# A four-layer diffusion trunk on one core: whole runs of small products, RG-LRU work moved off VectorE's conv, and another order for the trunk

## The chip, the cores and the metric

The kernel runs on one core of one Trainium2 chip. The core's engines work side by side, each on its own in-order queue: TensorE (PE, with its weight loads shown apart as PEld), VectorE (DVE), ScalarE (ACT), GpSimd (POOL), and SyncE (SP), which here issues most of the loads. The metric is the device time of one launch, in microseconds, as the median of several executions. A profile shows one execution.

## The reference, cut to what matters

A trunk of four layers over 512 latent and 256 context tokens of width 1024. Layer i has mixer i % 3: gated linear attention (GLA), windowed attention with a sink, RG-LRU, and GLA again. Each layer is modulated by shift, scale and gate from `c @ w_mod`.

```python
for i in range(4):
    kind, j, ctx_out = i % 3, i // 3, i < 3
    shift, scale, gate = split(silu(c) @ w_mod[i] + b_mod[i], 3)         # and the same for c_ctx
    h = rmsnorm(x, g_pre[i]) * (1 + scale) + shift                       # and hc from xc
    if kind == 0: y, yc = mixer_gla(h, hc, ...)     # q, k, v, z; decayed scores in both directions
    elif kind == 1: y, yc = mixer_swa(h, hc, ...)   # softmax over a window of 384, 256 context keys, a sink
    else: y, yc = mixer_rglru(h, hc, ...)           # conv of 4 taps, block-diagonal gates, linear scans
    x = x + gate * rmsnorm(y, g_post[i])            # and xc; every mixer's output is times silu(z), then @ w_out
```

RG-LRU is width 1280 in ten blocks of 128: `u = conv(h @ w_u)`; in each of two directions `r, i = sigmoid(u @ w_ra + b), sigmoid(u @ w_ri + b)`, `a = exp(-8 r softplus(-lam))`, `x = sqrt(1 - a*a) * i * u`, `h_t = a_t h_{t-1} + x_t`; the two directions are summed.

## The kernel before

All values are float32. A big product is made of three: each operand is split into a high part (`wh`, `Rh`, a cast on ScalarE at L265) and a low part (`wl`, `Rl`, a subtraction at L268 on VectorE, or every third time on GpSimd), and PE multiplies high by high, high by low and low by high with 128-row tiles and 256 or 512 columns (L384, L394, L790, L1027). Around them stand smaller products: the modulation (`mod_part`, L521: eight products for 256 columns of `w_mod`, each into 32 of the 128 output rows, so that four lie side by side), broadcasts of a gate (L579), transposes (L539, L635, L1494), GLA's decayed scores by levels of 1 to 128 tokens (L1065, 32 rows by 32 columns), and attention's probabilities times values (`heads`, L1508, 64 output rows for each of the two heads e of a pair).

The code is written for a scheduler that orders each engine's queue by priority (position in the program; `tc.high_priority(n)` moves an instruction ahead by n) and by its estimate of when each instruction can begin. Only the output product and norm of each layer (`finish`, from L731 on) have PE, ScalarE and VectorE in the order written. `weights` keeps two weight pieces converted ahead, in the order of a list per layer; `raw` tiles of 512 KB take each load. `background` puts the next layer's modulation, one piece of 256 columns after the other, between the parts of a layer.

Attention goes by 48 blocks (8 head pairs times 6 query tiles). `scores` makes products, maximum, exponential and normalised probabilities `pe` (VectorE L1465 to L1484, ScalarE L1475). `turn` transposes `pe` into PSUM (L1494) and copies it out to `pt` (L1499), e=0 on ScalarE and e=1 on VectorE. `heads` multiplies by the values. Scores run a block ahead of turns and turns a block ahead of heads; `fill` puts silu gate products (L394) between, by a credit of their length.

RG-LRU (`mix`, once for each block) does: conv on VectorE, one tap as a tensor_scalar (L1582) and three as scalar_tensor_tensor (L1584); split of u (cast L1590, subtraction L1591); load and split of the block's four gate weights (`wgh`, `wgl`); twelve products a stream (L1607); tanh, exponentials and a square root on ScalarE; combinations and scans on VectorE; the sum of the two directions on GpSimd (L1646). `finish` of this layer has two more weight rows of 128 (`wx`, loaded at L765) than the others.

Of the kernel before, what the change touches and what calls it, by code (L numbers as in the profile page):

```python
# [11 lines left out]
F32 = mybir.dt.float32  # L12
# [22 lines left out]
CTX0 = TL  # L35

# [40 lines left out]
def body(ctx: ExitStack, tc: tile.TileContext, I, out, layers=(0, 1, 2, 3)):  # L77
    nc = tc.nc
    V, S, G, PE = nc.vector, nc.scalar, nc.gpsimd, nc.tensor
# [426 lines left out]
    def mod_part(i, n, bank, pool, bufs):  # L506
# [12 lines left out]
        for k in range(KC):  # L519
            g = k % 4  # L520
            PE.matmul(  # L521
                ps[32 * g : 32 * g + 32, 0:256], sT[:, k, :], r2[k // 4][:, k % 4, :],
                start=(k < 4), stop=(k >= 4), skip_group_check=True,
            )
# [230 lines left out]
    def finish(i, kc, extra, last, final, xsrc, xdst):  # L755
# [4 lines left out]
        with phase(f"fin{i}", 6, 0) as fp:  # L760
            if kc > KC:
                wx = [fp.tile([P, kc - KC, D], F32R, name=n) for n in ("wxh", "wxl")]
                for k in range(kc - KC):
                    r = raw()
                    nc.sync.dma_start(r, I["c_w_out"][0, (KC + k) * P : (KC + k + 1) * P, :].rearrange("p (k n) -> p k n", k=4))  # L765
                    f = lambda t: t[:, k, :].rearrange("p (k n) -> p k n", k=4)
                    split(f(wx[0]), f(wx[1]), r)
# [13 lines left out]
            R = (Rh, Rl)  # L781

# [30 lines left out]
            def square(tt):  # L813
                rs[tt] = unit_rstd(fp, xs[tt], y[tt])
# [55 lines left out]
            def way(tt):  # L870

                residual(tt)
                yield
                square(tt)
                yield
                scale(tt)
                yield

# [6 lines left out]
            with tc.manual_schedule(engines={PE.engine, S.engine, V.engine}):  # L885
# [10 lines left out]
                scale(5)  # L896
                step((4, 5), 0)
                next(h)
# [37 lines left out]
    def gla(i, a, ctx_out):  # L936
# [3 lines left out]
        with phase(f"gla{i}") as mp:  # L940
# [96 lines left out]
            def levels(ls, q, Y, X, A):  # L1037
# [11 lines left out]
                small = {8: 0, 4: 1, 2: 2, 1: 3}  # L1049
                for n, L in enumerate(LEVELS):  # L1050
                    dims = ([2 * L, 16 // L], [T + L, 2], [1, L])
                    for gi, chunks in enumerate(groups if L < 128 else ()):
                        at = tl[gi][:, 0, :].rearrange("p (c t) -> p c t", t=P)
                        sml = tl[gi][:, 1, 0:480].rearrange("p (c l t) -> p c l t", l=5, t=32)
# [6 lines left out]
                        for ci, c in enumerate(chunks):  # L1061
                            for g in range(4):
                                t0 = c * P + 32 * g
                                r = slice(32 * g, 32 * g + 32)
                                mm = lambda o, k, x: PE.matmul(o, k, x, start=True, stop=True, skip_group_check=True)  # L1065
                                if L == 1:
                                    mm(sml[r, ci, 4, :], Y[:, 0, t0 : t0 + 32], q[:, t0 : t0 + 32])
                                if L <= 16:
                                    o = at[r, ci, 32 * g : 32 * g + 32] if L == 16 else sml[r, ci, small[L], :]
                                    mm(o, K[:, t0 - k0 : t0 - k0 + 32], view(Xf, t0, dims))  # L1070
                                elif L == 32:
                                    pl, o = (0, 32) if g % 2 == 0 else (1, -32)
                                    mm(
                                        at[r, ci, 32 * g + o : 32 * g + o + 32],
                                        Y[:, pl, t0 : t0 + 32],
                                        X[:, 1 - pl, t0 + o : t0 + o + 32],
                                    )
                                else:
                                    pl, o = (0, 64) if g < 2 else (1, 0)
                                    mm(  # L1080
                                        at[r, ci, o : o + 64],
                                        Y[:, pl, t0 : t0 + 32],
                                        X[:, 1 - pl, c * P + o : c * P + o + 64],
                                    )
# [214 lines left out]
    def attention(i):  # L1299
        with phase(f"att{i}", 6, 0) as mp:  # L1300
# [186 lines left out]

            def turn(b, qt, units, ps, keys):
                pt = mp.tile([P, 2, 640], F32, name="pt", tag="pt", bufs=2)
                for e in range(2):  # L1490
# [5 lines left out]
                    ev = V.tensor_copy if e else S.copy  # L1496
# [6 lines left out]
            def heads(b, qt, units, pt, keys):  # L1503
                po = units[0][0][0]
                kv = b // 2
                for m, t in enumerate(keys):
                    for e in range(2):
                        PE.matmul(  # L1508
                            po[64 * e : 64 * e + 64, 0:P], v[:, t, 64 * kv : 64 * kv + 64],
                            pt[:, e, m * P : (m + 1) * P],  # L1510
# [225 lines left out]
```

## Time and profile before

| | |
|---|---|
| median of 3 runs | 1557.77 us (1557.2 to 1561.75) |
| profiled execution | 1561.59 us |
| its span, first to last instruction | 1559.8 us |
| mean granted PE clock | 0.984 |
| PE busy | 1481.0 us, 95% |
| VectorE, ScalarE, GpSimd busy | 1031.4, 770.7, 238.4 us |
| DMA mean | 104 GB/s |

The profile puts the stages at about: start to 60 us (loads, first modulation); first GLA to 380; output product to 458; attention projections to 540 and attention blocks to 812; output product to 889; RG-LRU to 1138; output product to 1234; last GLA to 1509; last output product to the end. Idle time of an engine that is not the one waited for costs nothing. On PE an instruction's own duration overlaps the next one's, so what it costs is read from the start of one to the start of the next.

### The profile page before, as it was taken

The page shows a single profiled execution, that of the slowest core. Times are in us where ns is not written, and L with a number is a line of the kernel's source. Part 1 is how long each engine was busy: PE and PEld are TensorE (multiplying, and loading weights), DVE is VectorE, ACT ScalarE, POOL GpSimd, SP SyncE. Part 2 cuts the span into 40 slices and gives each one's busy share as a digit, 9 for nine tenths or more (in the row PEclk, how much of TensorE's full clock was granted, in tenths as well). Part 3 has the DMA queues.
Part 4 walks back from the last instruction along what each step waited for, and adds up shares of the span by engine and source line. Part 5 has one row for each costly group of instructions (what it writes and reads, how often), then busy time and mean ns, then how long its engine had stood idle before and what let it go on. Part 6 is the DMA issues. An engine that isn't in the chain of part 4 may idle for free.

```text
span 1559.8 us, 29164 instructions
## 1 busy us (share of the span) xinstructions
PE 1481.0 (95%) x11691; PEld 1222.5 (78%) x11691; DVE 1031.4 (66%) x1912; ACT 770.7 (49%) x1523; POOL 238.4 (15%) x322
## 2 busy tenths in 40 slices
PE   6998999999999999999999998899989999999998
PEld 3777787888878777888788776788867777888886
DVE  5575656576364398787882678999852566766754
ACT  5634352534252366565552556766732465255342
POOL 2211100112121200101001312212211201101011
PEclk8999999999999999999999999999999899999999
DMA  9431324112574532121225633221141233111122
GB/s 303 144 117 59 118 77 139 55 33 88 196 231 132 174 97 62 34 73 47 64 81 180 224 114 109 71 69 57 51 173 58 100 116 111 46 58 55 59 101 89
DMA packets 153047, 162.36 MB, mean 104 GB/s; under 512 B 12418, under 2 KB 141968, under 8 KB 152912
## 3 DMA queue, kind: packets, MB, share of 16 engines
q1 hardware_dynamic: 147456, 146.56, 30.5%
q10 hardware_dynamic: 5456, 13.94, 2.5%
q8 instruction: 92, 1.51, 0.4%
q14 instruction: 43, 0.35, 0.1%
HBM read 138.44 MB, written 11.53 MB: 96 GB/s over the span
## 4 chain that ended last, share of the span: by engine, by line
PE 51%; DVE 10%; ACT 5%; DMA 4%; issue 2%; POOL 1%; SPq 1%; POOLq 0%; ACTq 0%; DVEq 0%
PE mxt L790 14%; PE pjt L394 10%; PE pjt L384 7%; PE pjt L1027 4%; PE mxt L1508 3%; PE mxt L1494 2%; DMA raw<-in_w_mod_dram 2%; PE sct L1607 2%; PE mxt L521 2%; PE mxt L1456 1%; PE mxt L1176 1%; DMA bb<-in_b_mod_dram 1%; PE mxt L1439 1%; DVE wl L268 1%; PE mxt L1148 1%
## 5 line engine op out<-in xcount | busy, mean ns | idle before, releaser
L384 PE MATMUL pjt<-Rh,wh 128*128 128x256 f32 (+1 forms) x592 | 199.9, 339 | 7.3 <-DVE Rh L646 5.5
L384 PE MATMUL pjt<-Rl,wh 128*128 128x256 f32 (+1 forms) x592 | 199.0, 337 | 2.1 <-DVE Rl L647 2.0
L384 PE MATMUL pjt<-Rh,wl 128*128 128x256 f32 (+1 forms) x592 | 197.7, 335 | 0.0
L265 ACT CAST wh<-raw 128x1024 fp32r<-128x1024 f32 x118 | 122.4, 1051 | 121.6 <-PE mxt L790 35.2
L268 DVE TENSOR_TENSOR wl<-raw,wh 128x1024 fp32r<-128x1024 f32 x102 | 128.3, 1266 | 78.7 <-ACT wh L265 78.2
L394 PE MATMUL pjt<-Rh,wh 128*128 128x512 f32 (+1 forms) x448 | 161.1, 360 | 0.0
L394 PE MATMUL pjt<-Rl,wh 128*128 128x512 f32 (+1 forms) x448 | 160.7, 359 | 0.0
L394 PE MATMUL pjt<-Rh,wl 128*128 128x512 f32 (+1 forms) x448 | 158.9, 355 | 0.0
L790 PE MATMUL mxt<-wh,Rh 128*128 128x512 f32 x352 | 140.5, 402 | 4.0 <-ACT wh L265 4.0
L790 PE MATMUL mxt<-wl,Rh 128*128 128x512 f32 x352 | 138.7, 394 | 0.0
L790 PE MATMUL mxt<-wh,Rl 128*128 128x512 f32 x352 | 138.6, 394 | 0.0
L384 PEld LDWEIGHTS pjt<-Rh,wh 128*128 128x128 f32 x592 | 113.0, 191 | 23.1 <-DVE Rh L646 7.1
L384 PEld LDWEIGHTS pjt<-Rl,wh 128*128 128x128 f32 x592 | 113.5, 192 | 16.6 <-DVE Rl L647 4.1
L384 PEld LDWEIGHTS pjt<-Rh,wl 128*128 128x128 f32 x592 | 113.5, 192 | 12.3 <-issue 0.8
L1027 PE MATMUL pjt<-wh,Rh 128*128 128x256 f32 x384 | 112.5, 293 | 0.0
L1027 PE MATMUL pjt<-wl,Rh 128*128 128x256 f32 x384 | 110.2, 287 | 0.0
L1027 PE MATMUL pjt<-wh,Rl 128*128 128x256 f32 x384 | 110.1, 287 | 0.0
L394 PEld LDWEIGHTS pjt<-Rh,wh 128*128 128x128 f32 x448 | 85.0, 190 | 12.5 <-issue 4.5
L394 PEld LDWEIGHTS pjt<-Rh,wl 128*128 128x128 f32 x448 | 85.0, 190 | 11.0 <-issue 3.2
L394 PEld LDWEIGHTS pjt<-Rl,wh 128*128 128x128 f32 x448 | 85.1, 190 | 9.7 <-issue 2.4
L1475 ACT ACTIVATE pe<-mxt,mxs 128x256 f32<-128x256 f32 (+2 forms) x128 | 70.5, 554 | 34.2 <-DVE mxs L1467 29.9
L790 PEld LDWEIGHTS mxt<-wh,Rh 128*128 128x128 f32 x352 | 67.3, 192 | 19.8 <-ACT wh L265 4.8
(299 smaller groups left out, 3530.1 us busy)
## 6 DMA issues: line engine op xcount, KB each, us to landing
rawp<-in_w_mod_dram SPq DMA_DIRECT2D x48, 512.0 KB, 5.8
raw<-in_w_mod_dram SPq DMA_DIRECT2D x48, 512.0 KB, 3.6
raw<-in_a_w_in_dram SPq DMA_DIRECT2D x32, 512.0 KB, 3.5
raw<-in_b_w_in_dram SPq DMA_DIRECT2D x20, 512.0 KB, 4.7
raw<-in_c_w_in_dram SPq DMA_DIRECT2D x20, 512.0 KB, 3.4
xd<-x SPq DMA_DIRECT2D x18, 512.0 KB, 2.6
raw<-in_a_w_out_dram SPq DMA_DIRECT2D x16, 512.0 KB, 3.6
x<-xd ACTq DMA_DIRECT2D x16, 512.0 KB, 9.1
```

The source lines that it names most:

```text
L265: S.copy(h, x)
L268: e.tensor_tensor(l, x, h.bitcast(F32), op=ALU.subtract)
L384: PE.matmul(ps, w[u][:, k, c0 : c0 + P], R[v][:, k, t0 : t0 + n], start=(k == 0 and u + v == 0), stop=(k == KC - 1 and u == 1),)
L394: PE.matmul(ps, w[u][:, k, c0 : c0 + P], R[x][:, k, t0 : t0 + n], start=(k == 0 and u + x == 0), stop=(k == KC - 1 and u == 1),)
L521: PE.matmul(ps[32 * g : 32 * g + 32, 0:256], sT[:, k, :], r2[k // 4][:, k % 4, :], start=(k < 4), stop=(k >= 4), skip_group_check=True,)
L790: PE.matmul(ps, l[:, tt * P : (tt + 1) * P], r, start=(k == 0 and u + v == 0), stop=(k == kc - 1 and u == 1),)
L1027: PE.matmul(ps[:, n, :], R[u][:, k, tt * P : (tt + 1) * P], w[x][:, k, :], start=(k == 0 and u + x == 0), stop=(k == KC - 1 and u == 1),)
L1148: PE.matmul(ps[:, pl * GDV : (pl + 1) * GDV], k[x][:, pl * P : (pl + 1) * P], v[y][:, order[pl][m], :], start=(n == 0), stop=(n == 2),)
L1475: S.activation(p[:, o : o + w], u[e][:, :w], AF.Exp, bias=nm, scale=0.125, accum_out=den[:, n : n + 1],)
L1494: PE.transpose(u[e][:, c * P : (c + 1) * P], ps[e][:, m * P : (m + 1) * P], ident)
L1508: PE.matmul(po[64 * e : 64 * e + 64, 0:P], v[:, t, 64 * kv : 64 * kv + 64], pt[:, e, m * P : (m + 1) * P], start=(m == 0), stop=(m == len( ...
L1607: PE.matmul(ps[:, t0 : t0 + nn], wg[a][:, n, :], x[c][:, p0 : p0 + nn], start=(q == 0), stop=(q == 2),)
```

## The change

The whole body becomes one named block that is ordered by another model of the engines' timelines. The eight modulation products, one level's GLA products and one block's `heads` are each put under `high_priority`, the modulation with the later half of its weights first, GLA's groups and heads' keys in reverse order. `turn` copies both e of a block out on one engine, ScalarE and VectorE in turn from block to block. In `mix`, the first tap and the cast of u go from VectorE to ScalarE, the sum of the directions from GpSimd to VectorE; gate weights are loaded and split one block ahead; while RG-LRU runs, splits are kept off GpSimd. In `finish` the two extra weight rows are loaded after the first output weights instead of ahead of everything, with their split on VectorE; in the one finish that has no fill, one step is drawn a place earlier. An unused function falls away.

```diff
+BURST = 300
...
+    ctx.enter_context(tc.block(name="trunk", schedule_with_timeline_sim=True))
...
-    def split(h, l, x):
+    def split(h, l, x, share=True):
...
-        e = G if cnt[0] % 3 == 0 and not keep_pool else V
+        e = G if share and cnt[0] % 3 == 0 and not keep_pool else V
...
-        for k in range(KC):
-            g = k % 4
...
+        with tc.high_priority(BURST + 200):
+            for n, k in enumerate((*range(4, KC), *range(4))):
+                g = k % 4
+                PE.matmul(
+                    ps[32 * g : 32 * g + 32, 0:256], sT[:, k, :], r2[k // 4][:, k % 4, :],
+                    start=(n < 4), stop=(n >= 4), skip_group_check=True,
+                )
...
-            if kc > KC:
-                wx = [fp.tile([P, kc - KC, D], F32R, name=n) for n in ("wxh", "wxl")]
...
+            def load_extra():
...
+                    split(f(wx[0]), f(wx[1]), r, False)
...
                 w = weights(f"o{kh}")
+                if kc > KC and not kh:
+                    load_extra()
...
+                if not fill:
+                    next(h)
                 step((4, 5), 0)
-                next(h)
+                next(h, None)
...
+                    with tc.high_priority(BURST):
+                        for gi, (chunks, K) in reversed(list(enumerate(Ks))):
+                            products(L, dims, tl[gi], chunks, K)
...
-                    ev = V.tensor_copy if e else S.copy
+                    ev = V.tensor_copy if turns[0] % 2 else S.copy
...
+                with tc.high_priority(BURST):
+                    for m in reversed(range(len(keys))):
+                        for e in (1, 0):
...
+        def gate_weights(b):
+            r = raw()
...
+            split(*gw[b], r[:, :, 0:P])
...
-            V.tensor_scalar(u[:, m], up[:, m], cw[:, 20 + b : 21 + b], cb[:, b : b + 1], op0=ALU.mult, op1=ALU.add)
...
+            with tc.high_priority(120):
+                S.activation(u[:, m], up[:, m], AF.Identity, bias=cb[:, b : b + 1], scale=cw[:, 20 + b : 21 + b])
...
+                S.copy(uh[:, m], u[:, m])
...
+            if b + 1 < RB:
+                gate_weights(b + 1)
...
-            G.tensor_tensor(o, hs[0], hs[1], op=ALU.add)
+            V.tensor_tensor(o, hs[0], hs[1], op=ALU.add)
...
+        keep_pool.append(1)
+        gate_weights(0)
```

In the order's rows a form such as `64x128` is rows by columns of the product, `x7` seven in a row. Line numbers after differ from those before: L521 is L525 after, L394 is L396, L1439 and L1456 (scores) are L1452 and L1469, L1494 is L1510, L1508 is L1526, L579 is L583, L1027 is L1029, L1065 is L1057.

PE in the first GLA, where a modulation piece stands among the products for v (L1027); before:

```order
L1027 MATMUL pjt<-wl,Rh 128x256
L1027 MATMUL pjt<-wh,Rl 128x256
L521 MATMUL mxt<-raw,sT 32x256
L579 MATMUL mxt<-mh,sel 128x256
L521 MATMUL mxt<-raw,sT 32x256 x3
L1027 MATMUL pjt<-wh,Rh 128x256
L1027 MATMUL pjt<-wl,Rh 128x256
L1027 MATMUL pjt<-wh,Rl 128x256
```

and after:

```order
L1029 MATMUL pjt<-wh,Rh 128x256
L1029 MATMUL pjt<-wl,Rh 128x256
L1057 MATMUL sct<-q,Y 32x32
L525 MATMUL mxt<-raw,sT 32x256 x8
L1057 MATMUL sct<-q,Y 32x32
L1029 MATMUL pjt<-wh,Rl 128x256
L1029 MATMUL pjt<-wh,Rh 128x256
```

The products of a piece stand together, with one level product each side; before, they stood in pieces of 4, 1, 3 and the like.

PE in the middle of attention; before:

```order
L394 MATMUL pjt<-Rh,wh 128x512
L1508 MATMUL mxt<-pt,v 64x128
L1494 MATMUL mxt<-ident,pe 128x128 x5
L394 MATMUL pjt<-Rl,wh 128x512
L394 MATMUL pjt<-Rh,wl 128x512
L394 MATMUL pjt<-Rh,wh 128x512
L394 MATMUL pjt<-Rl,wh 128x512
L1508 MATMUL mxt<-pt,v 64x128 x2
L1494 MATMUL mxt<-ident,pe 128x128 x2
L1508 MATMUL mxt<-pt,v 64x128 x7
L1439 MATMUL mxt<-khi,q_6103 128x384
L1439 MATMUL mxt<-klo,q_6103 128x384
```

and after:

```order
L396 MATMUL pjt<-Rh,wh 128x256
L396 MATMUL pjt<-Rl,wh 128x256
L1526 MATMUL mxt<-pt,v 64x128 x10
L1510 MATMUL mxt<-ident,pe 128x128 x2
L1469 MATMUL mxt<-khi,q_6104 128x256
L1469 MATMUL mxt<-klo,q_6104 128x256
L1469 MATMUL mxt<-khi,q_6110 128x256
L1469 MATMUL mxt<-klo,q_6110 128x256
L1510 MATMUL mxt<-ident,pe 128x128 x8
L396 MATMUL pjt<-Rh,wl 128x256
L396 MATMUL pjt<-Rh,wh 128x256
```

A block's heads are one run of ten, and transposes gather in eights.

PE at the end of attention in the new order, from the last fill product on:

```order
L396 MATMUL pjt<-Rh,wl 128x512
L1510 MATMUL mxt<-ident,pe 128x128 x4
L1452 MATMUL mxt<-khi,q_8324 128x384
L1452 MATMUL mxt<-klo,q_8324 128x384
L1458 LDWEIGHTS idb
L1458 MATMUL mxt<-band,idb 128x2x128
L1526 MATMUL mxt<-pt,v 64x128 x10
L1469 MATMUL mxt<-khi,q_8324 128x256
L1469 MATMUL mxt<-klo,q_8324 128x256
L1469 MATMUL mxt<-khi,q_8330 128x256
L1469 MATMUL mxt<-klo,q_8330 128x256
L1510 MATMUL mxt<-ident,pe 128x128 x6
```

and at the end of attention before:

```order
L394 MATMUL pjt<-Rh,wh 128x512
L1494 MATMUL mxt<-ident,pe 128x128 x8
L394 MATMUL pjt<-Rl,wh 128x512
L394 MATMUL pjt<-Rh,wl 128x512
L394 MATMUL pjt<-Rh,wh 128x512
L1494 MATMUL mxt<-ident,pe 128x128 x2
L394 MATMUL pjt<-Rl,wh 128x512
L394 MATMUL pjt<-Rh,wl 128x512
L394 MATMUL pjt<-Rh,wh 128x512
L394 MATMUL pjt<-Rl,wh 128x512
L394 MATMUL pjt<-Rh,wl 128x512
L1508 MATMUL mxt<-pt,v 64x128 x18
```

The last fill product (L396) stands before the last 46 transposes and 34 score products; before, L394 stood up to the last heads.

SyncE's queue in the first 45 us; before:

```order
L275 DMA rawp<-in_a_w_g_dram 128x8x16 x2
L510 DMA rawp<-in_w_mod_dram 128x4x256 x8
L228 DMA rawp<-in_a_w_in_dram 128x4x128 x4
L510 DMA rawp<-in_w_mod_dram 128x4x256 x4
L302 DMA gpt<-in_a_w_g_dram 16x512 x3
L228 DMA raw<-in_a_w_in_dram 128x4x256 x2
L560 DMA gb<-in_g_post_dram 128x256
L564 DMA bb<-in_b_mod_dram 128x256
```

and after:

```order
L277 DMA rawp<-in_a_w_g_dram 128x8x16 x2
L512 DMA rawp<-in_w_mod_dram 128x4x256 x5
L304 DMA gpt<-in_a_w_g_dram 16x512 x3
L230 DMA raw<-in_a_w_in_dram 128x4x256 x2
L564 DMA gb<-in_g_post_dram 128x256
L568 DMA bb<-in_b_mod_dram 128x256
L512 DMA rawp<-in_w_mod_dram 128x4x256 x3
L230 DMA rawp<-in_a_w_in_dram 128x4x128 x4
L512 DMA rawp<-in_w_mod_dram 128x4x256 x4
```

The loads of `gpt`, of 512 KB pieces of `a_w_in`, of `gb` and of `bb` stand ahead of the last seven of `w_mod`.

## Rows read from the trace of the kernel before

**Rows 1.** Windows: length, busy us by engine, PE clock, DMA share, GB/s.

```profile
20.00:45.00 25.00, 20.09 (x161) 10.76 (x150) 16.32 (x39) 13.07 (x26) 6.46 (x6) 0.80 1.07 326
540.00:812.00 272.00, 268.76 (x2063) 218.12 (x2062) 223.10 (x686) 169.54 (x530) 20.00 (x12) 1.00 0.22 60
960.00:1138.00 178.00, 169.37 (x933) 146.99 (x933) 167.97 (x199) 127.34 (x148) 42.88 (x31) 0.98 0.22 66
1157.80:1164.60 6.80, 5.95 (x13) 4.29 (x14) 2.04 (x2) 1.83 (x2) 2.38 (x1) 0.50 0.48 154
```

**Rows 2.** PE timeline, products at L521 and L790: start, us, passes.

```profile
426.50 0.39 PE L790 MATMUL mxt<-wh,Rl 128*128 128x512 f32 x1
426.81 1.07 PE L521 MATMUL mxt<-rawp,sT 128*32 128x256 f32 x16
427.81 0.50 PE L790 MATMUL mxt<-wh,Rh 128*128 128x512 f32 x1
428.16 0.40 PE L790 MATMUL mxt<-wl,Rh 128*128 128x512 f32 x1
...
511.46 0.63 PE L521 MATMUL mxt<-raw,sT 128*32 128x256 f32 x6
512.02 0.39 PE L394 MATMUL pjt<-Rh,wh 128*128 128x256 f32 x1
```

**Rows 3.** PE timeline, attention: start, us, operation, passes.

```profile
620.66 0.43 PE L1508 MATMUL mxt<-pt,v 128*64 128x128 f32 x2
621.02 0.50 PE L394 MATMUL pjt<-Rl,wh 128*128 128x512 f32 x1
621.35 0.39 PE L394 MATMUL pjt<-Rh,wl 128*128 128x512 f32 x1
621.58 0.39 PE L394 MATMUL pjt<-Rh,wh 128*128 128x512 f32 x1
...
625.79 0.38 PE L1494 MATMUL mxt<-ident,pe 128*128 128x128 f32 x2
626.10 0.66 PE L1508 MATMUL mxt<-pt,v 128*64 128x128 f32 x8
626.69 0.50 PE L394 MATMUL pjt<-Rh,wh 128*128 128x512 f32 x1
...
631.26 0.38 PE L1494 MATMUL mxt<-ident,pe 128*128 128x128 f32 x2
631.39 0.47 PE L394 MATMUL pjt<-Rh,wl 128*128 128x512 f32 x1
631.71 0.39 PE L394 MATMUL pjt<-Rh,wh 128*128 128x512 f32 x1
```

**Rows 4.** Lines of VectorE, 540 to 812: busy us, mean ns | idle.

```profile
L1499 DVE COPY pt<-mxt 128x256 f32<-128x256 f32 (+1 forms) x64 | 32.7, 519 | 10.5 <-PE mxt L1494 9.0 <-ACT den L1481 1.1 <-ACT OG L1517 0.2
```

**Rows 5.** Lines of VectorE, 889 to 1138, as rows 4.

```profile
L1584 DVE SCALAR_TENSOR_TENSOR u<-up,cwb,u 128x773 f32<-128x773 f32 x30 | 35.2, 1174 | 0.7
L1582 DVE TENSOR_SCALAR u<-up,cwb 128x773 f32<-128x773 f32 x10 | 8.2, 822 | 0.1
L1590 DVE CAST uh<-u 128x773 fp32r<-128x773 f32 x10 | 5.6, 558 | 2.0 <-PE sct L1607 1.9
```

**Rows 6.** Waits of PE, whole span: us, times, longest.

```profile
PE sct L1065 <- ACT K L1060: 6.4, 6, 2.0
PE mxt L790 <- ACT wh L265: 4.0, 1, 4.0
PE sct L1607 <- POOL wgl L268: 3.6, 1, 3.6
```

**Rows 7.** Tile u, 889 to 1138: ns min/median/max.

```profile
L1584 DVE SCALAR_TENSOR_TENSOR u<-up,cwb,u x30: 1010/1023/2494, 911.7 to 1083.2; 128x773 f32<-128x773 f32 x30
```

**Rows 8.** Chain that ended last: start, us, what.

```profile
1148.11 9.41 DMA raw<-in_c_w_out_dram
```

More of the change, by code (lines that the diff above doesn't have):

```diff
@@ L518, in mod_part @@
         ps = bank()
-        for k in range(KC):
-            g = k % 4
[L521 to L524, printed above, removed]
+        with tc.high_priority(BURST + 200):
[5 more added lines that the diff above has]
+                )
         return ps[:, 0:256]
@@ L760, in finish @@
         with phase(f"fin{i}", 6, 0) as fp:
-            if kc > KC:
-                wx = [fp.tile([P, kc - KC, D], F32R, name=n) for n in ("wxh", "wxl")]
[L763 to L767, printed above, removed]
             parts = [(k, 0, nt) for k in range(KC - 2)]
@@ L781, in finish @@
             R = (Rh, Rl)
+            wx = []
+            def load_extra():
+                wx.extend(fp.tile([P, kc - KC, D], F32R, name=n) for n in ("wxh", "wxl"))
+                for k in range(kc - KC):
+                    r = raw()
+                    nc.sync.dma_start(r, I["c_w_out"][0, (KC + k) * P : (KC + k + 1) * P, :].rearrange("p (k n) -> p k n", k=4))
+                    f = lambda t: t[:, k, :].rearrange("p (k n) -> p k n", k=4)
+                    split(f(wx[0]), f(wx[1]), r, False)
             def product(w, kh, ch, tt, ps):
@@ L1060, in levels @@
                             S.copy(K[:, :kn], view(Yf, k0, ([2 * L, kn // (2 * L)], [T + L, 2], [1, L])))
[L1061 to L1084, printed above, removed]
+                        else:
+                            K = None
+                        Ks.append((chunks, K))
+                    with tc.high_priority(BURST):
+                        for gi, (chunks, K) in reversed(list(enumerate(Ks))):
+                            products(L, dims, tl[gi], chunks, K)
                     if L < 128:
@@ L1486, in scores @@
                 return b, qt, units, ps, loc + [4, 5]
+            turns = [0]
             def turn(b, qt, units, ps, keys):
+                turns[0] += 1
                 pt = mp.tile([P, 2, 640], F32, name="pt", tag="pt", bufs=2)
@@ L1505, in heads @@
                 kv = b // 2
[L1506 to L1510, printed above, removed]
-                            start=(m == 0), stop=(m == len(keys) - 1), skip_group_check=True,
-                        )
+                with tc.high_priority(BURST):
+                    for m in reversed(range(len(keys))):
+                        for e in (1, 0):
+                            PE.matmul(
+                                po[64 * e : 64 * e + 64, 0:P], v[:, keys[m], 64 * kv : 64 * kv + 64],
+                                pt[:, e, m * P : (m + 1) * P],
+                                start=(m == len(keys) - 1), stop=(m == 0), skip_group_check=True,
+                            )
                 o = OG[:, b, qt * P : (qt + 1) * P]
@@ L1576, in gates @@
                 V.tensor_tensor(ex[1][:, m, :], h, ex[0][:, m, :].bitcast(F32), op=ALU.subtract)
+        gw = {}
+        def gate_weights(b):
+            r = raw()
+            for n, (wn, d) in enumerate((("c_w_ra", 0), ("c_w_ri", 0), ("c_w_ra", 1), ("c_w_ri", 1))):
+                nc.sync.dma_start(r[:, n, 0:P], I[wn][0, d, b])
+            gw[b] = [mp.tile([P, 4, P], F32R, name=n, tag=n) for n in ("wgh", "wgl")]
+            split(*gw[b], r[:, :, 0:P])
         def mix(b, up):
@@ L1661, in rglru @@
         gates(RB // 2 - 1, outs)
+        keep_pool.clear()
         finish_args[0] = (RB, ex)
```

60 lines of the change are left out of this document (37 added, 23 removed).

## The prediction

> **What bounds the kernel now.** I read the page from the outside in: the busy shares first, then the windows by stage, then what PE waits for, then PE's own timeline. TensorE is busy for 95% of the span. The windows say the same of the long stages: in the attention stage PE is busy 268.76 of 272 us, in the RG-LRU stage 169.37 of 178 us with VectorE at 167.97 us beside it [rows 1]. So almost everywhere PE's in-order queue sets the end, and in RG-LRU a second engine stands close behind it.
>
> A busy PE is not an efficient PE, and the timeline shows it. I take the time from one row's start to the next row's start. Two like products of 512 columns follow each other in 0.23 us (621.35 to 621.58) [rows 3]. Products of another shape break this. Eight modulation products of 32 columns take 1.00 us as one run (426.81 to 427.81); three of them alone already take 0.56 us (511.46 to 512.02; x6 counts two passes each) [rows 2]. That fits 0.13 us for a run and 0.43 us for each four begun: 0.56 for up to four, 0.99 for eight. The big product ahead of such a run takes 0.31 us instead of 0.23 (426.50 to 426.81), the first behind it 0.35 (427.81 to 428.16) [rows 2]. The products of probabilities with values (heads) take 0.36 us for one (620.66 to 621.02) and 0.59 for four (626.10 to 626.69), so 0.13 a run and 0.23 for each two begun; the first big product behind them takes 0.33 [rows 3]. Two transposes cost 0.31 us ahead of heads (625.79 to 626.10), but 0.13 ahead of a big product (631.26 to 631.39), whose own time is then 0.32 (to 631.71) [rows 3].
>
> **The change part by part.** The matrix products are the same in number and shape; what moves is their order.
>
> *Runs on PE.* I counted runs in both orders. Modulation products: 384 in 82 runs become 384 in 46 (all of 8 or 16), and the fours begun fall from 117 to 96: 36 x 0.13 + 21 x 0.43 = -13.7 us. Steps from a big product to a 32-column one fall from 115 to 82, and as many back: 33 x (0.08 + 0.12) = -6.6. Heads: 352 in 77 runs become 42, pairs begun fall from 197 to 176: 35 x 0.13 + 21 x 0.23 = -9.4. Steps from transposes straight to heads fall from 51 to 13: 38 x 0.18 = -6.8. Steps from heads to big products fall from 53 to 33: 20 x 0.10 = -2.0. Steps from transposes to big products rise from 123 to 141: 18 x 0.09 = +1.6. Together -36.9 us. All of it lies on PE's queue. Finer pricing, by what stands on both sides of each product, gives about -44, which I keep as the far end.
>
> The row at 631.39 shows a big product 0.09 us late behind transposes of the same 128x128 shape [rows 3]. The Trainium skill, TensorEngine Tiling (Array Packing), Key Properties, puts the cost of a switch on a change of the tiling mode, not of the tile. By that alone the +1.6 would be nothing and the sum 1.6 us lower; the row decides for 1.6.
>
> *What attention gives back.* The new order runs the gate products that fill attention earlier. Priced at the steps above, 114 of 138 us of fill are done when 192 of the 352 transposes are, against 86 us before. After the last fill product (third order excerpt), 46 transposes, 34 score products and their heads remain. So from there 22 of 48 blocks run with 24 us of fill instead of 52. PE's own work for a block is (268.8 - 138) / 48 = 2.7 us, hence about 82 us for PE over these blocks. VectorE does 223.1 us in this stage, 4.65 us a block at most [rows 1]; a part of it prepares q, k and weights, so I estimate 4.0 to 4.65, or 88 to 102 us. VectorE would then be late by 6 to 20 us. I take +13, between the ends; 0 if it enters the tail with a lead.
>
> *Start-up.* The excerpt of SyncE's queue shows three small loads, two of 512 KB, and two of 128 KB moved ahead of the last seven w_mod loads, 1.4 MB in all. At the 326 GB/s of that stretch [rows 1] the last w_mod load lands 4.2 us later. Some of its products can trade places with others: +3, between 0 and 4.2.
>
> *GLA levels.* All copies K of a level now precede its products. That can remove waits such as the six, 6.4 us, on K [rows 6]; or, where two levels of a head now stand close together, add as many. I cost it at 0, with ends of -6 and +6.
>
> *RG-LRU.* VectorE loses ten first taps (8.2 us) and ten casts (5.6 us) [rows 5]. It gains ten sums. Their nearest row is the conv step of the same size with two inputs, 1.02 us in the median [rows 7]: +10.2. It gains seven gate-weight splits of 512 columns, by width 0.68 each: +4.8; and three weight splits of 1024, 1.35 each: +4.0. That is +5.2. Against it, the conv steps average 1174 ns [rows 5] with a median of 1023 [rows 7], and the slow ones are those beside a working GpSimd: 30 x 0.15 = 4.5 us that fall away with GpSimd's sums and splits. Other two-input operations suffer alike; at the same 13% on some 60 us more I take 8. Net -7 us, between +1 and -13. ScalarE gains 20 instructions, 0.56 to 1.02 us each by the same rows, 11 to 20 us; at 127 of 178 us [rows 1] it has the room, and loading gate weights one block ahead removes PE's 3.6 us wait for them on GpSimd [rows 6]. I take -7 for the stage. Since VectorE is close to the bound there, some 3 us of the shorter runs of this stage can't show: +3.
>
> *Finish of layer 2.* PE waits 4.0 us for wh on ScalarE [rows 6]; behind it stands a load of c_w_out that took 9.41 us on the chain [rows 8], and then 6.8 us pass at a granted clock of 0.50, which is 1.2 GHz [rows 1], so 3.4 us are lost. With the o0 and o1 loads ahead of the extra rows that wait goes: -7.4 if entirely; I take -6, since the extra rows must still arrive in time.
>
> The eviction of turn, ScalarE and VectorE in alternation instead of side by side, keeps each engine's total; its latency is a rival below.
>
> **Sum.** -36.9 + 13 + 3 + 0 - 7 + 3 - 6 = -31 us. The profiled execution took 1561.59 us, its span 1559.8; so 1530.7 for a like execution. It lay 3.8 us above the median 1557.77, which I take off: 1527 us.
>
> **The rivals.** *VectorE keeps its lead.* If softmax is ahead when the fill runs out, the 13 us are not given back, and start-up hides its loads: 1527 - 16 = 1511; with the finer price of the runs, -7 more, 1504. For it: VectorE has 49 us free in the stage [rows 1]. Against: it can only lead as far as its few buffers reach.
>
> *Attention gives back all its gain, and RG-LRU stands still.* Of the -36.9 some 20 lie in attention (heads, steps around them, a few modulation runs). If VectorE is 20 us late there, not 13, RG-LRU trades VectorE for ScalarE at no gain (+7), and levels cost 6: 1527 + 7 + 7 + 6 = 1547. For it: the new order's tail, plainly bare of fill.
>
> *Slower: turn's evictions hold up the heads.* A turn has 2.67 copies on average, of 519 ns on VectorE [rows 4]. One engine in series needs 1.4 us where two needed 0.7. Heads are hoisted in bursts and may arrive too soon; each of 48 groups then waits up to 1.4 us, 66 us in all, for 1593. The kernel turns slower from 0.75 us a group. Against it: I work out a median of 2.3 us of PE work between a block's transposes and its heads in the new order, with only ten groups below 1.4 us, about 5 us of waiting that the overlap with the other half of the turn shortens. The Trainium skill, TensorEngine Tiling (Array Packing), Performance Considerations, advises both ScalarE and VectorE for emptying PSUM; no run so far shows one turn on one engine.
>
> *The change does not do what it says* is excluded for the runs: the order shows the modulation runs whole. For the waits it is part of the second rival.
>
> **How the numbers follow.** The forecast has 0.53 (about 1514 to 1541), the first rival 0.20 (1504 to 1514), the second 0.18 (1541 to 1555), the third 0.05, anything else 0.04. The range from 1503 to 1550 leaves out the slow cases and a part of the second rival. A measurement of this kernel can tell about 0.3%, 4.7 us, from no change: faster means below 1553.1. The second rival puts 0.04 above that, so: faster 0.87, same 0.06, slower 0.07.
>
> **What would show it.** PE's modulation products in runs of x16 (two passes each) at 1.00 us, and PE busy well below 1481 us at nearly the same share. In attention, waits of PE on VectorE or ScalarE in the last 90 us of the stage, 6 to 20 us. The first w_mod waits some 3 us later. No wait for wgl on GpSimd, conv steps at about 1.02 us on average, ScalarE near 84% in RG-LRU. No 9 us load on the chain at the last finish of layer 2. The prediction is wrong if new waits on pt exceed 20 us, if the w_mod bursts wait for the second half of their weights more than the present runs do, or if the half-clock stretches grow.

## The result and the profile after

The changed kernel takes 1641.07 us in the median (1637.52 to 1641.96) against 1557.49 us for the kernel before: 1.053 times as long, 95% interval 1.050 to 1.056. The forecast was 1527 us, with a range of 1503 to 1550. The span of the profiled execution is 1639.1 us, 79.3 more than before.

The page's first lines after the change (busy us, share of the span, instructions), then those of the same kernel without the block, which comes below:

```profile
PE 1487.6 (91%) x11691; PEld 1249.1 (76%) x11691; DVE 1021.9 (62%) x1913; ACT 787.7 (48%) x1541; POOL 201.1 (12%) x301
```

```profile
PE 1441.5 (95%) x11691; PEld 1207.9 (79%) x11691; DVE 1014.0 (67%) x1913; ACT 786.6 (52%) x1543; POOL 187.9 (12%) x301
```

PE's share fell from 95% to 91%, and yet it is busy 6.6 us longer than the 1481.0 us of before. PE waits more, and more of its work falls into stretches in which its granted clock is at the lower level (0.50, which is 1.2 GHz). This is the table by stage; stages are cut at the first product of the next one on PE's timeline, and each cell gives length / PE idle / time at a granted clock of 0.50, in us:

| stage | before | changed | changed, without the block |
|---|---|---|---|
| start and first GLA | 380.5 / 31.0 / 17.1 | 415.7 / 59.8 / 64.9 | 374.0 / 34.5 / 17.1 |
| attention, projections | 81.1 / 4.9 / 3.4 | 82.4 / 7.1 / 3.4 | 82.2 / 8.6 / 3.4 |
| attention, blocks | 273.4 / 3.2 / 0.0 | 298.9 / 32.6 / 23.9 | 262.2 / 5.7 / 0.0 |
| RG-LRU | 249.1 / 15.0 / 6.8 | 249.5 / 17.3 / 17.1 | 237.1 / 9.0 / 3.4 |
| output of layer 2 | 95.0 / 5.9 / 10.2 | 85.3 / 0.7 / 0.0 | 87.9 / 2.4 / 0.0 |
| last GLA | 275.7 / 11.6 / 10.2 | 301.2 / 27.0 / 35.2 | 272.9 / 12.7 / 6.8 |

The three other stages (output products, 198 us in all) hardly move. In the changed kernel PE idles 144.5 us against 71.7, and 147 us pass at the lower clock against 48. Not all of that time is filled: PE is busy in 116 us of it against 44. If each busy us there loses about half (rows below: 0.21 us for a product instead of 0.12), the clock costs 36 us more. Then 73 us of waits and 36 of clock make 109 us, and the span is 79 longer. The 29 us between are, by this estimate, what shorter runs saved.

The windows of the changed kernel for the stages that lost and of RG-LRU (length, busy us of PE, PEld, DVE, ACT, POOL, then PE clock, DMA share, GB/s), with one stretch of the first GLA; the second row of [rows 1] answers to 575 to 874:

```profile
79.00:416.00 337.00, 296.11 (x3308) 254.03 (x3308) 197.07 (x312) 131.49 (x236) 39.81 (x68) 0.92 0.25 77
575.00:874.00 299.00, 266.29 (x2062) 223.30 (x2061) 230.46 (x697) 172.17 (x532) 20.90 (x12) 0.96 0.21 58
951.00:1201.00 250.00, 232.69 (x1356) 197.90 (x1355) 203.02 (x273) 185.58 (x228) 12.43 (x42) 0.97 0.26 81
1286.00:1588.00 302.00, 274.98 (x2585) 236.49 (x2584) 190.02 (x297) 136.56 (x232) 39.56 (x69) 0.94 0.23 72
265.20:285.70 20.50, 12.70 (x222) 9.01 (x209) 12.44 (x22) 7.46 (x13) 0.00 (x0) 0.50 0.52 164
```

and of the kernel before for its first GLA stage, RG-LRU and its last GLA stage:

```profile
68.00:381.00 313.00, 297.65 (x3365) 252.09 (x3364) 200.04 (x319) 135.23 (x244) 37.65 (x68) 0.99 0.28 86
889.00:1138.00 249.00, 233.95 (x1355) 197.06 (x1354) 223.13 (x276) 168.88 (x208) 58.60 (x62) 0.99 0.27 80
1233.00:1509.00 276.00, 264.37 (x2584) 225.93 (x2583) 188.01 (x295) 133.96 (x233) 35.20 (x69) 0.98 0.25 75
```

These are the largest waits of PE in the whole span after the change (us in total, times, longest). The wait on K was 6.4 us in [rows 6]; the other two rows of that group, the output product's wait for wh and the gates' for wgl, are gone (one of 3.2 us on wgh has come):

```profile
PE mxt L525 <- DMA raw<-in_w_mod_dram: 19.2, 8, 4.0
PE sct L1057 <- ACT K L1091: 10.7, 7, 4.0
PE mxt L681 <- DVE xp L675: 9.8, 1, 9.8
PE mxt L1526 <- DVE pt L1515: 8.6, 3, 4.1
PE mxt L1526 <- ACT pt L1515: 7.2, 4, 2.6
PE pjt L525 <- DMA rawp<-in_w_mod_dram: 5.4, 1, 5.4
```

and two rows of the kernel before that answer to the first and the fourth:

```profile
PE mxt L521 <- DMA raw<-in_w_mod_dram: 7.7, 8, 1.8
PE mxt L1508 <- DVE pt L1499: 0.2, 1, 0.2
```

No row is large. There are many, on loads, on ScalarE and on VectorE alike. The 9.8 us on xp are no new wait: they are the time to PE's first product, and before PE came to the same transposes no earlier (10.58 us against 9.81), after waits of 6.9 and 3.0 us. A piece of PE's timeline in the first GLA shows how they hang together (start, us, operation, passes, in brackets the idle time ahead and what ended it):

```profile
264.50 0.86 PE L1057 MATMUL sct<-X,K 128*32 128x32 f32 x48 [0.95 <-ACT K L1091]
267.49 1.94 PE L525 MATMUL mxt<-raw,sT 128*32 128x256 f32 x16 [2.13 <-DMA raw<-in_w_mod_dram]
269.36 0.69 PE L543 MATMUL mxt<-ident,mp 128*128 128x128 f32 x2
269.98 0.87 PE L1057 MATMUL sct<-X,K 128*32 128x32 f32 x48
274.12 1.94 PE L525 MATMUL mxt<-raw,sT 128*32 128x256 f32 x16 [3.28 <-DMA raw<-in_w_mod_dram]
276.61 0.87 PE L1057 MATMUL sct<-X,K 128*32 128x32 f32 x48
279.87 0.80 PE L1029 MATMUL pjt<-wh,Rh 128*128 128x256 f32 x2 [2.40 <-ACT wh L267]
282.00 0.41 PE L1029 MATMUL pjt<-wh,Rh 128*128 128x256 f32 x1
282.21 0.41 PE L1029 MATMUL pjt<-wl,Rh 128*128 128x256 f32 x1
...
285.91 0.28 PE L1029 MATMUL pjt<-wl,Rh 128*128 128x256 f32 x1
286.03 0.28 PE L1029 MATMUL pjt<-wh,Rl 128*128 128x256 f32 x1
```

Within 20 us four groups of products stand each behind something that is not there yet: a copy K, twice a load of w_mod, a weight cast. The run of eight modulation products takes 1.87 us (267.49 to 269.36) where it took 1.00 in [rows 2], and a product for v takes 0.21 us (282.00 to 282.21) until 285.7, and 0.12 us behind it (285.91 to 286.03). The window row above gives the clock of that stretch as 0.50, the 1.2 GHz level.

SyncE's waits between 235 and 280 us show what the loads stood behind:

```profile
SPq L512 <- PE mxt L525: 43.1, 3, 41.5
```

For 41.5 us the queue held a load whose buffer a modulation product had still to release, and that product stood in PE's order at 260.88 us. The next four loads of w_mod were issued from 261.58 on, and the weights for v behind them. The kernel before has such waits in its first GLA too, 31.0 us the longest; but its longest wait of PE on `raw` of w_mod is 1.8 us.

### The profile page after: what moved, and what is told of

Same layout as the page of the kernel before. It is cut to its first block, busy times and chain, and to the rows that moved or that the text cites. A ratio compares the mean times of both kernels' runs of the same rounds, so it can differ in the third digit from the quotient of the medians.

```text
span 1639.1 us, 29081 instructions
## 1 busy us (share of the span) xinstructions
PE 1487.6 (91%) x11691; PEld 1249.1 (76%) x11691; DVE 1021.9 (62%) x1913; ACT 787.7 (48%) x1541; POOL 201.1 (12%) x301
## 5 line engine op out<-in xcount | busy, mean ns | idle before, releaser
L270 DVE TENSOR_TENSOR wl<-raw,wh 128x1024 fp32r<-128x1024 f32 x105 | 133.9, 1293 | 94.5 <-ACT wh L267 94.3
L396 PE MATMUL pjt<-Rh,wh 128*128 128x512 f32 (+1 forms) x448 | 159.2, 355 | 4.9 <-ACT xq L1394 3.5
L396 PE MATMUL pjt<-Rh,wl 128*128 128x512 f32 (+1 forms) x448 | 157.5, 352 | 0.8 <-DVE wl L270 0.8
L396 PE MATMUL pjt<-Rl,wh 128*128 128x512 f32 (+1 forms) x448 | 157.6, 352 | 0.0
L1029 PE MATMUL pjt<-wh,Rh 128*128 128x256 f32 x384 | 115.0, 301 | 9.3 <-ACT wh L267 4.8
L1029 PE MATMUL pjt<-wh,Rl 128*128 128x256 f32 x384 | 113.9, 297 | 0.0
L1029 PE MATMUL pjt<-wl,Rh 128*128 128x256 f32 x384 | 113.8, 297 | 0.0
L396 PEld LDWEIGHTS pjt<-Rh,wh 128*128 128x128 f32 x448 | 86.6, 193 | 16.1 <-ACT xq L1394 4.3
L396 PEld LDWEIGHTS pjt<-Rh,wl 128*128 128x128 f32 x448 | 86.5, 193 | 10.6 <-DVE wl L270 1.2
L396 PEld LDWEIGHTS pjt<-Rl,wh 128*128 128x128 f32 x448 | 86.6, 193 | 9.4
L1029 PEld LDWEIGHTS pjt<-wh,Rh 128*128 128x128 f32 x384 | 78.2, 204 | 11.1 <-ACT wh L267 5.1
```

Source lines behind the costliest of these rows:

```text
L396: PE.matmul(ps, w[u][:, k, c0 : c0 + P], R[x][:, k, t0 : t0 + n], start=(k == 0 and u + x == 0), stop=(k == KC - 1 and u == 1),)
L1029: PE.matmul(ps[:, n, :], R[u][:, k, tt * P : (tt + 1) * P], w[x][:, k, :], start=(k == 0 and u + x == 0), stop=(k == KC - 1 and u == 1),)
```

## The experiments

All times are medians; ratios are to the kernel before on the same chip, with 95% intervals.

**Which part costs.** Four kernels take the change apart. `no_block` leaves out one line of the changed kernel:

```diff
-    ctx.enter_context(tc.block(name="trunk", schedule_with_timeline_sim=True))
```

> The changed kernel without the named block: the order comes from the model of before, all else stays. If the hoisted runs (modulation, GLA levels, heads) make TensorE wait by themselves, it stays near the changed kernel's 1641 us (1610 to 1645). If the other model of the timeline is the cause, the waits go and the shorter runs show: 1515 to 1545.

Measured: 1525.75 us, 0.981 (0.979 to 0.984). `block_only` puts that line into the kernel before and does nothing else:

> The kernel before with nothing but the named block. If the hoisted runs are the cause, it stays within 10 us of 1557. If the model of the timeline is, it is 1610 to 1640, with PE waits and half-clock stretches in both GLA layers and in attention.

Measured: 1643.80 us, 1.056 (1.053 to 1.058). The first line of its page:

```profile
PE 1513.3 (92%) x11691; PEld 1247.7 (76%) x11691; DVE 1037.5 (63%) x1912; ACT 772.5 (47%) x1521; POOL 247.5 (15%) x322
```

It is long in the stages in which the changed kernel is: the first GLA 410.8 us, the attention blocks 302.7, the last GLA 301.5. PE idles 120.7 us, 49 more than before; by the estimate above the clock costs 24 us more and PE's own work, in this other order, 9. `no_bursts` keeps the block and takes back the hoisted runs:

```diff
-        with tc.high_priority(BURST + 200):
-            for n, k in enumerate((*range(4, KC), *range(4))):
+        for k in range(KC):
...
-                    with tc.high_priority(BURST):
-                        for gi, (chunks, K) in reversed(list(enumerate(Ks))):
...
-                with tc.high_priority(BURST):
-                    for m in reversed(range(len(keys))):
```

> The changed kernel with modulation, GLA levels and heads written as before (no hoisting), block, RG-LRU, finish and the eviction by turns kept. Hoisted runs as the cause: 1540 to 1565. The model of the timeline as the cause: 1620 to 1650.

Measured: 1623.74 us, 1.043 (1.041 to 1.045). `lru_finish_only` is the kernel before with the RG-LRU and `finish` edits:

> The kernel before with only the RG-LRU edits and the moved load of the extra output weights. The stage from the first output product of layer 2 to its end took 85.3 us in the changed kernel against 95.0, the RG-LRU stage 249.5 against 249.1. If these two add up alone, 1545 to 1550; if RG-LRU was held back by the other parts, down to 1535.

Measured: 1544.18 us, 0.992 (0.990 to 0.994). So the loss is that one line's: 87 us on the kernel before, 115 on the changed one. It is the model, not the block: with `schedule_with_timeline_sim=False` in the same block, the program holds the same instructions in the same order on all five queues as without a block, so that kernel was not timed. The rest of the change gains, and the model turns one part of this gain round: the hoisted runs and the eviction by turns bring 18 us without it (1544.18 to 1525.75), and the hoisted runs cost 17 with it (1623.74 to 1641.07). The estimate from above, taken between these last two, says how: the runs save PE 37 us of its own work, but it waits 37 us more (144.5 against 107.9), and the clock costs another 17 (116 busy us at the lower clock against 81).

**What each of the other parts is worth**, taken back one at a time from `no_block`. `nb_no_mod` takes back the modulation runs as above.

> The changed kernel without the block, with the modulation products written as before. By the prediction's price of their runs (13.7 us for the pieces, 6.6 for the steps around them, some 3 of it hidden in RG-LRU) 1540 to 1546 against 1525.75. If a whole run gives back what it saves by waiting for both halves of its weights, it stays within 5 us of 1526.

Measured: 1529.38 us, 0.983 (0.980 to 0.986). The interval overlaps that of `no_block`. The runs did shorten: in 79 runs with 115 fours begun, against 47 and 96, which is 12.3 us by the prediction's price, and 4 more for the steps. But PE idles 7.6 us longer in the first GLA with whole runs (34.5 against 26.9), 2.3 in attention's projections and 1.8 in the last GLA. The waits on w_mod of `no_block`, then of `nb_no_mod`:

```profile
PE mxt L524 <- DMA raw<-in_w_mod_dram: 9.6, 10, 2.2
PE mxt L524 <- DMA rawp<-in_w_mod_dram: 4.1, 1, 4.1
```

```profile
PE mxt L522 <- DMA raw<-in_w_mod_dram: 7.4, 7, 2.0
PE mxt L522 <- DMA rawp<-in_w_mod_dram: 2.5, 2, 2.1
```

A part of the give-back stands in these rows, 3.8 us; the rest is idle time behind other releasers in the same stages. By the estimate from above whole runs save 13 us of PE's own work, 12 more of idle time give that back, and what is left of the difference is mostly clock. `nb_no_heads` takes back the hoisting in `heads`.

> The same without the block, with the heads products not hoisted. The prediction's price of their runs is 9.4 us, 6.8 for transposes ahead of them and 2 behind them: 1540 to 1546. If VectorE takes the stage back, within 5 us of 1526.

Measured: 1543.86 us, 0.991 (0.988 to 0.994), 18 us slower than `no_block`, as priced (the three head terms of the prediction add up to 18.2); the attention stage goes from 262.2 to 278.5 us with PE idle for 5.7 and 5.5. Of 47 steps from transposes straight to heads one is left in `no_block`, and runs of heads fall from 81 to 48. `nb_no_lev` takes back the GLA products.

> The same without the block, with the GLA level products written as before. The prediction costed this part at 0 with ends of -6 and +6, so 1520 to 1532; if the dealt-out products are what speeds up the first GLA stage (374.0 us against 376.6 with the RG-LRU edits alone), 1530 or more.

Measured: 1531.12 us, 0.984 (0.981 to 0.986). The intervals overlap; the two GLA stages are 4.2 and 3.1 us longer than in `no_block`, so a gain of some 5 us is possible and not shown. PE's own work differs by 2 us; most of the rest is time at the lower clock, 44 us against 31, and the granted clock of one kernel differs as much from run to run (0.983 to 0.989 in four runs of `no_block`). `nb_old_ev` takes back the eviction by turns.

```diff
-                    ev = V.tensor_copy if turns[0] % 2 else S.copy
+                    ev = V.tensor_copy if e else S.copy
```

> The same without the block, with both engines emptying one turn as before. If a turn on one engine delays the heads (the rival, up to 1.4 us for each of 48 groups), this is faster by 5 to 20 us, 1506 to 1521, and the waits on pt go. If the distance hides it, 1524 to 1528.

Measured: 1527.48 us, 0.982 (0.979 to 0.985): no difference. Which engine empties a turn does not matter without the block. `nb_mod_dma` hoists the loads of w_mod as far as their products.

```diff
+            with tc.high_priority(BURST + 200):
+                nc.sync.dma_start(
...
```

> The changed kernel without the block, with the loads of the modulation weights hoisted as far as their products. Removing the hoisted modulation products cost 4 us where their runs alone are priced at 16; if the rest is given back in waits for the second half of the weights (16.6 us in all there, 12.4 in the kernel without hoisting), earlier loads take 4 to 10 us off: 1516 to 1522. If the loads are held by their buffers, 1524 to 1530.

Measured: 1527.90 us, 0.981 (0.978 to 0.983). The wait on w_mod into `raw` stays: 9.1 us in ten waits, against 9.6 in ten. Priority is not what holds these loads; they still wait for buffers that modulation products release. SyncE's row from 80 to 410 us, of `no_block`, reads

```profile
SPq L511 <- PE mxt L524: 64.9, 6, 32.0
```

and in `nb_mod_dma` the same wait is 60.4 us in seven, 28.1 the longest.

**Where the finer model costs.** The model that the block's option switches on is called the finer one here. The first try put a block around one layer of `no_block`.

```diff
-            attention(i)
+            with tc.block(name="att", schedule_with_timeline_sim=True):
+                attention(i)
```

> The changed kernel without the block around the trunk, with a block on the finer model around the attention layer alone. If that model's order costs time in every stage whose TensorE work is nearly gapless, by its own order there, the attention stage goes from 262 us to 285 to 300 and the whole to 1550 to 1565, and the GLA and RG-LRU stages stay as they are. If the loss came from what the model did at the start or to the loads ahead, 1526 to 1535.

> The same with the block around the attention layer on the model of before. It prices the edge of a block by itself: 1526 to 1540 by every theory, and the attention blocks near 262 us.

Measured: 1562.07 us with the finer model and 1561.36 with that of before; the stage of the attention blocks 293.1 and 287.3 us. The expectation of the control was missed: a block around one layer costs 36 us without any change of the model. That work on either side of its edges can't mix is the likely reason, which no run shows. Inside these edges the finer model costs 6 us in the stage of the blocks, where it costs 37 around the whole trunk (298.9 against 262.2); the pair can't tell why. `lru_true` does the same around RG-LRU.

> The changed kernel without the block around the trunk, with a block on the finer model around RG-LRU alone. In the kernel with nothing but the trunk's block this stage went from 249.1 to 240.3 us, so the finer order may help where VectorE is the bound: 1515 to 1526. If the loss hits every stage, or the edges cost, 1530 to 1545.

Measured: 1624.87 us, far above both expectations; the RG-LRU stage takes 331.0 us with PE idle for 76.6. Without a control it can't be divided between edges and model.

The second try fixes PE's queue, so that only the other queues differ: `ma_false` and `ma_true` have PE in the code's order through the attention layer, without the trunk's block and with it.

```diff
-            attention(i)
+            with tc.manual_schedule(engines={PE.engine}):
+                attention(i)
```

> The changed kernel without the block, with TensorE's queue in the attention layer in the order of the code; the model orders all else. It is the control of the next. The attention blocks of the code's order run scores, transposes and heads without fill inside a block: 265 to 300 us for the stage, 1530 to 1570 in all.

> The changed kernel with its block, with TensorE's queue in the attention layer in the order of the code. If the finer model costs time by TensorE's order, the attention stage is within 5 us of the control's, the GLA stages stay long (about 412 and 301 us). If it costs time by the order of VectorE's, ScalarE's and the loads' queues, the stage is 15 to 30 us longer than the control's.

Measured: 1614.21 and 1722.46 us. From the first score product to the last of heads both have the same 1796 products in the same order. The control missed its expectation, in all and in the stage, which takes 340.2 us; it takes 368.3 under the finer model. That is 28 us longer, as expected of the other queues, with PE idle 14 us more and 43 us more at the lower clock. In the blocks PE's waits end on VectorE and ScalarE alone, on no load; those on ScalarE grow from 8 to 19 us. `mg_false` and `mg_true` do the same through the GLA layers too.

> Without the block, TensorE's queue in the order of the code in the GLA layers and attention. Control of the next. GLA in the code's order waits for vector work between levels: 400 to 480 us for the first GLA stage.

> With the block, TensorE's queue in the order of the code in the GLA layers and attention. TensorE's order as the cause: both GLA stages within 8 us of the control's. The other queues as the cause: the first GLA stage 20 to 40 us longer than the control's, the last 15 to 30 us.

Measured: 1743.47 and 1812.77 us; attention 343.3 and 372.5, 29 us again; the first GLA stage 454.0 and 471.7, the last 317.7 and 340.9, so 18 and 23 us, where the free orders differ by 42 and 28. The 18 us lie between the two expectations. In GLA some 70 of the first 2755 products still differ at their place. So with PE's products in the same order, or nearly, the finer model still costs 70 us over these three stages, where it costs 107 with free orders; in the first GLA it is less than half. What costs these 70 us is the order of the queues that feed PE. The two figures come from different kernels, so PE's own order may have a part in the rest, and how much is open.

One such place, in `ma_true`. PE waits twice within one turn, first until the other half's exponential has read the PSUM tile that the transposes write, then for that half's normalised probabilities:

```profile
604.82 0.69 PE L1510 MATMUL mxt<-ident,pe 128*128 128x128 f32 x2 [1.97 <-ACT pe L1488]
607.51 1.33 PE L1510 MATMUL mxt<-ident,pe 128*128 128x128 f32 x5 [2.00 <-DVE pe L1497]
```

VectorE has the last maximum that the next exponential needs at 601.15; ScalarE is at two weight casts and a copy of a projection, and VectorE itself at the low part of a weight:

```profile
600.99 0.16 DVE L1480 SCALAR_TENSOR_TENSOR mxs<-mxs 128x1 f32<-128x1 f32 x1
602.35 1.23 DVE L270 TENSOR_TENSOR wl<-raw,wh 128x1024 fp32r<-128x1024 f32 x1 [0.53 <-ACT wh L267]
```

```profile
601.26 2.00 ACT L267 CAST wh<-raw 128x1024 fp32r<-128x1024 f32 x2 [0.42 <-PE pjt L396]
603.16 0.58 ACT L1394 COPY xq<-pjt 128x512 f32<-128x512 f32 x1
603.63 0.58 ACT L1488 ACTIVATE pe<-mxt,mxs 128x384 f32<-128x384 f32 x1
```

The exponential starts 2.5 us after its input is there, and PE's 1.97 us of waiting end with the exponential behind it. In the control the exponential at this place waits 1.98 us for VectorE, and PE's waits in this turn are 0.98, 0.66 and 0.47 us, 2.1 us in all against 4.0. One such place does not show what makes up the 28 us. The last pair tests whether the casts are the cause: `mc_false` and `mc_true` are the two kernels with the weight casts of the attention layer on GpSimd.

```diff
-        S.copy(h, x)
+        (G.tensor_copy if att_on else S.copy)(h, x)
```

> As ma_false (no block, TensorE's attention queue in the order of the code), with the high-part casts of the weights that fall into the attention layer moved from ScalarE to GpSimd. Control of the next: the attention stage near ma_false's 340 us, within 12 us.

> As ma_true (block, the same TensorE order in attention, 368 us there), with the weight casts of the attention layer on GpSimd. In the trace of ma_true two casts in a row (2.0 us) stand ahead of the exponentials that the next transposes wait for. If such casts on ScalarE are what the finer model's order costs, the stage comes within 10 us of the control's. If the rest of the order of VectorE and ScalarE costs it, it stays 20 to 30 us above it.

Measured: 1629.65 and 1721.19 us; the blocks' stage 355.6 and 363.8 us, the projections ahead of it 94.5 and 101.4 (92.7 and 91.9 in the pair before). The gap in the blocks shrinks from 28 to 8 us, but the control rose by 15 us, beyond the 12 expected, and the projections now differ by 7: over both, 27 us became 15. The gap shrank because the control got 17 us longer over both stages; the kernel with the block got 5 us longer, not shorter. So nothing here shows that the casts on ScalarE are what the finer model's order costs. Which instructions on the other queues cost it stays open.

## Why the prediction was wrong

**The step that failed** is the one that is hardly written there: the change of the model itself has no term in the sum. The prediction read the new order on PE, counted its runs, and then priced the queue as if operands came as before, but for one place each: +13 in attention's tail, +3 at the start, 0 (-6 to +6) for the GLA levels. A new order is a new set of waits at every product, on five queues at once. The one line of the block alone, put into the kernel before, costs 87 us (`block_only`). In the changed kernel the waits came to 73 us more and the clock to about 36: attention's blocks idle 29 us more, and the two GLA stages, costed at 0, 29 and 15. No rival had this mechanism; the slow one was sought in turn's evictions. But the prediction's last sentence names three signs of being wrong, and all three came. Waits on pt are 21.8 us in all (0.2 before), waits on w_mod 26.5 (12.3), and the time at the lower clock is 147 us (48).

**The switching term** (-36.9, at the far end -44) had the right sign and was too large: by the estimate above shorter runs saved 29 us in the changed kernel and 30 in `no_block`. In `no_block`, whose runs are other ones, its parts separate: heads 18 us, as priced; the modulation runs some 4 us where their price was 20, since 12 us of new waits give back most of what PE saves. The prediction named such a mechanism at its end, bursts that wait for the second half of their weights, and put no price on it; 3.8 us of the 12 end on w_mod.

**Attention's tail.** In the changed kernel no fill product stands in the last 28.0 us of the stage (3.0 before), and PE idles 11.5 us in the last 90 us of it (1.2 before), all behind VectorE and ScalarE, where the prediction's sign was 6 to 20. So this term (+13) came about as forecast, although its own sum has a slip: 22 blocks of 2.7 us and 24 us of fill are 84 us, not 82. But the stage's first quarter, 75 us, idles 15.2 us, with 17 at the lower clock, and there the prediction had nothing.

**Start-up** came as forecast. Up to the first level product PE idles 18.9 us against 15.6, so 3.3 more where +3 was; the largest new wait is 5.4 us for a w_mod load. The stretch is 10.9 us longer because 54 more passes of other products stand in it.

**GLA levels.** Costed at 0: without the block they bring 3 to 4 us in each GLA stage (not shown beyond the interval); with it, the waits on K grow from 6.4 to 10.7 us, which is the model's doing and not the hoisting's (10.4 in `no_bursts`).

**RG-LRU** came as worked out in the kernels without the block; in the changed kernel the stage stayed at 249.5 us, with 17 us at the lower clock. The conv steps' row of `no_block`, which answers to the first of [rows 5]:

```profile
L1614 DVE SCALAR_TENSOR_TENSOR u<-up,cwb,u 128x773 f32<-128x773 f32 x30 | 30.6, 1020 | 3.7 <-ACT u L1612 3.2
```

Their mean falls from 1174 to 1020 ns (1023 forecast, the median of [rows 7]). The Trainium skill, GPSIMD Engine Reference, 1. Specifications, says that GpSimd shares its SBUF interfaces with VectorE and contends with VectorE instructions of two SBUF inputs; these rows agree, with GpSimd busy 9.4 us in the stage instead of 58.6. The mean was raised by few steps: before, four of the 30 took 1.77 to 2.49 us, each with GpSimd at work during 0.95 to 1.67 us of it, and each was longer than the others' 1.02 us by about as much, less 0.2; two steps with 0.2 and 0.35 us of GpSimd's work in them were not slowed. The stage takes 241.7 us in `lru_finish_only`, 7.4 less, where -7 was the term. The finish of layer 2 takes 88.6 there against 95.0: 6.4, where -6 was. (Its 3.4 us for the clock count the whole 6.8 us; PE is busy in 5.95 of them [rows 1], so 3.0 was the price.)

**The turn's evictions**, the slow rival, cost nothing that can be measured without the block: `nb_old_ev` is 0.1% from `no_block`. Under the block PE's waits on pt are 21.8 us in the changed kernel, 12.2 in `block_only` (both engines, no hoisting) and 11.7 in `no_bursts` (in turns, no hoisting). So the evictions by turns alone add none there, and 10 us come with the hoisted runs. The hoisted runs with both engines were not run under the block. The Trainium skill, TensorEngine Tiling (Array Packing), Performance Considerations, advises both engines for emptying PSUM; taking them in turn keeps to that over two turns, and no run here shows a price of it by itself.

Without the block the change comes to 1525.75 us, near the forecast of 1527. That agreement is partly luck, since this is another order than the one that was read. Its fill stands until 2.1 us before the end of attention, and PE idles 5.7 us in the blocks, so the +13 has nothing to act on; in return the switching term came to 30 us instead of 36.9, and new waits gave back most of what the modulation runs saved.

## What to carry to other kernels

When a change hands the whole program to another ordering model, that is the change, and its price is not in the instructions: run that line alone before anything else. The order of PE's products tells its runs before anything is timed, here within some 8 us of 37. It does not tell its waits, unless the producers of each product are followed through their own queues. Where PE is busy for 95% of the time there is little to hide new waits behind, and they cost again in the clock: 36 us beside 73 us of waits here. Measure hoisted work under the model that it will ship with: the same hoisting brought 18 us under one model and cost 17 under the other.

The version to keep is the changed kernel without the block: 0.981 (0.979 to 0.984) of the kernel before.

## What the runs showed of the hardware

Time at the lower clock grew faster than idle time: with 73 us more of waits came 99 us more at a granted clock of 0.50, and PE was busy in 72 of these 99. In the first GLA one stretch holds for 20.5 us, and waits of 2.13, 3.28 and 2.40 us lie in it. In `ma_true`, PE idles only 14 us more in attention than in its control, and 43 us more pass at the lower clock: the clock's loss does not follow from the sum of the waits alone.
